# Seven products instead of eight for the last eight blocks of the down-projection

## The chip, the cores and the metric

The kernel runs on one core of a Trainium2 chip. The metric is the device time of one launch in microseconds (us); the cost of an edit is read from one profiled execution. The engines are TensorE (PE in the profile, PEld for its weight loads), VectorE (DVE), ScalarE (ACT), GpSimd (POOL) and SyncE (SP). SP computes nothing: it issues nearly all transfers of the stretch discussed here, in order, and waits in front of each until what it needs is done.

## The reference

A one-layer decoder trunk on 1024 tokens of width 1024. The change lies in the last matrix product, its operand preparation and the final norm.

```python
def conv_ffn(xn, w_up, conv_w, conv_b, w_down):
    u = xn @ w_up                                  # (1024, 5632)
    ...                                            # causal depthwise conv, width 3
    gate, val = jnp.split(c, 2, axis=-1)
    return (jax.nn.silu(gate) * val) @ w_down      # (1024, 2816) @ (2816, 1024)
...
x = x + conv_ffn(rmsnorm(x, norm_ffn_w), ...)
return rmsnorm(x, norm_final_w)
```

## The kernel before

Activations lie transposed: 128 channels on the partitions, tokens along the free axis, in two halves of 512 tokens (`hf`). The hidden layer has NF = 22 blocks of 128 channels; the down-projection sums over these 22 blocks into eight output tiles of 128 channels (`m`), kept in SBUF as `x3` with the residual already in it.

Every fp32 product is made of three matmuls in the fp32r format: an operand is split into a high part (a cast on ScalarE, line L799 for activations, L145 or L122 for weights) and a low part (a subtraction on VectorE, L800, L147, L123), and high x high, high x low and low x high are added in PSUM. So each operand costs one ScalarE and one VectorE instruction, and each block product of 512 tokens three matmuls.

Where eight blocks can be paired into 2 x 2 quarters (output tiles m and m+4, token halves 0 and 1), the kernel replaces eight quarter products by seven, with sums of operands (`product`, L873 to L888). The weight sums S1 to S4 are made by GpSimd from two loaded tiles (`sum_pair`, L98 to L104), the differences T1 to T4 of the activations by VectorE (`sums_h`, L1016 to L1022).

`down` has three stretches, in program order:

1. Blocks 0 to 5 directly (matmuls of L1118).
2. Blocks 6 to 13 in seven products. A first pass over m = 0 to 3 makes A11 B11 into a PSUM tile `y` and A12 B21 (lines L880, L882, L886 to L888, called in L1144 and L1145). A second pass over the same m makes S1 T1, S2 T2, S4 B22, A22 T4 and S3 T3, twelve matmuls each; S2 T2 and S3 T3 are added on top of `y`, and between those two VectorE must read `y` (L1158), because its two partial sums go to different places.
3. Blocks 14 to 21 directly (`mms`, L1091): all eight m for half 0, then for half 1; the last two m of half 1 in quarters of 256 tokens. After each product `evac` adds it to `x3` (L1178), squares it (L1181), sums the squares (L1183) and multiplies by the norm's weight (L1184); `last_norm` makes the final norm.

The order of work is the program's, engine by engine: each engine runs its instructions strictly in the order in which they stand. A tile pool with n buffers makes a load wait until the tile n places before it has been read. Important pools: `hr` (raw activations, 9 buffers), `h` (split activations, 28), `raw` (raw weights, 3), `wh`, `wl`, `sh`, `sl` (split weights, 2 each) and the PSUM tiles `d` and `y` (4 each). Split activations of the last eight blocks are made during the second pass, four for each m (`load_h`), and weights are loaded two items ahead of their use (`next_w`).

Of the kernel before, what the change touches and what calls it, by code (L numbers as in the profile page):

```python
# [17 lines left out]
P = 128  # L18
# [12 lines left out]
N1 = 6  # L31
LPAD, RPAD = 288, 480
# [11 lines left out]
class Trunk:  # L44
# [24 lines left out]
    def ahead(self, n):  # L69
        while len(self.wq) < n and self.wsrc and (self.wsrc[0][1] != "pair" or self.uw):  # L70
# [4 lines left out]
            elif nk == "rest":  # L75
                self.sums["A22"] = self.load_w(src[1][:, 4:8], 4)
                self.wq.append(self.sums)
            elif nk == "pair":
# [28 lines left out]
    def split_pair(self, g, v, sa, sb, skip=0, end=4):  # L107
# [22 lines left out]
        self.pin, self.after = False, None  # L130
        return ops
# [74 lines left out]
    def run(self):  # L206
        nc, tc = self.nc, self.tc
        with ExitStack() as ctx:
# [21 lines left out]
            self.hd = self.dp.tile([NF, P, T], F32, name="hd")  # L230
            self.yd = self.dp.tile([8, P, T], F32, name="yd")
# [15 lines left out]
    def plan(self):  # L247
# [21 lines left out]
        n, n2 = N1 // 2, NF - N1 - 8  # L269
# [6 lines left out]
        src += [(self.w_dn[m, :, N1 + 8:, :], n2) for _ in range(2) for m in range(KC)]  # L276
# [595 lines left out]
    def product(self, ps, a, b, ks=range(4), first=True, last=True, skip=False, low_last=False):  # L872
# [4 lines left out]
        if low_last:  # L877
            for n, k in enumerate(ks):
                for i, x in enumerate(self.B[b, k]):
                    nc.tensor.matmul(ps, ah[:, k, :], x, start=first and n == i == 0, stop=False, skip_group_check=skip)  # L880
            for n, k in enumerate(ks):
                i = nc.tensor.matmul(ps, al[:, k, :], self.B[b, k][0], start=False, stop=last and n == len(ks) - 1, skip_group_check=skip)  # L882
            return i
        for n, k in enumerate(ks):
            bh, bl = self.B[b, k]
# [184 lines left out]
    def down(self):  # L1070

        nc, tc = self.nc, self.tc
        with ExitStack() as ctx:
# [64 lines left out]
            assert not preps  # L1138
            ys = []
# [10 lines left out]
            late = [(hf, j) for hf in range(2) for j in range(N1 + 8, NF)]  # L1150
            for m, y in enumerate(ys):
# [16 lines left out]
                for _ in range(4):  # L1168
                    hf, j = late.pop(0)
                    self.load_h(j, hf)  # L1170
            acc = self.tl(self.uw, [P, 2, H2], "sh")
            js = range(N1 + 8, NF)
            q = H2 // 2

            def evac(ps, m, hf, a=0, b=H2):

                x = x3[:, m, hf * H2 + a:hf * H2 + b]
                tt(x, x, ps, ALU.add)  # L1178
                sum_ = acc[:, hf, a:b]
                sq = sum_ if m == 0 else self.tl(self.uw, [P, b - a], "sl")  # L1180
                nc.scalar.activation(sq, x, AF.Square)  # L1181
                if m and (m < KC - 1 or not hf):
                    tt(sum_, sum_, sq, ALU.add)  # L1183
                nc.scalar.mul(x, x, self.vecs[:, C_NO + m:C_NO + m + 1])  # L1184
                return sq

            tail = []
            for hf in range(2):
                for m in range(KC if hf == 0 else KC - 2):
# [116 lines left out]
```

## Time and profile before

| | |
|---|---|
| median of 3 runs (lowest to highest) | 1350.27 us (1348.31 to 1350.51) |
| profiled execution, its own time | 1349.12 us |
| its span | 1347.3 us |
| PE busy | 1328.9 us, 99% of the span |
| VectorE, ScalarE, GpSimd busy | 77%, 46%, 35% |
| first pass, blocks 6 to 13 | 1170.78 to 1192.37 us |
| second pass | 1192.37 to 1246.94 us |
| last eight blocks, first matmul | 1246.94 us |

The span is the time between the first and last instruction; 1.8 us lie around it. The granted TensorE clock is full. A busy PE in these pages means that matmuls follow each other without a gap; the time of a stretch is then the number of its matmuls times their spacing, and only a change in that number, or a wait that opens a gap, moves the end.

### The profile page before, as it was taken

How to read it: one execution, taken by the hardware profiler on the slowest of the kernel's cores; microseconds unless marked ns; L12 is line 12 of the kernel's file. 1: busy time of each engine (PE TensorE's matmuls, PEld its weight loads, DVE VectorE, ACT ScalarE, POOL GpSimd, SP SyncE). 2: the span in 40 equal slices, each digit the busy share in tenths (PEclk: the TensorE clock that was granted, in tenths of full speed). 3: DMA queues.
4: the chain of work that ended last, by engine and by line, in shares of the span. 5: the costliest groups of instructions: out<-in, count | busy, mean ns of one | idle time of the engine just before them, and what ended most of it. 6: DMA issues, size and time to landing. Idle time of an engine off the chain costs nothing.

```text
span 1347.3 us, 17300 instructions
## 1 busy us (share of the span) xinstructions
PE 1328.9 (99%) x6304; PEld 1104.6 (82%) x6304; DVE 1036.0 (77%) x1557; ACT 616.1 (46%) x1003; POOL 470.6 (35%) x349
## 2 busy tenths in 40 slices
PE   7999999999999999999999999999999999999997
PEld 6888888888888777878888888888888888888887
DVE  7847775289899875465678999999999987986454
ACT  8432232276667665333454444444444434433343
POOL 0336552000102124641455555565555511231011
PEclk9999999999999999999999999999999999999998
DMA  6423443866553235334433222222222238552342
GB/s 257 146 105 150 148 156 141 251 175 188 141 149 130 87 114 207 129 110 155 141 107 96 79 79 94 78 94 74 83 94 74 86 136 315 197 180 67 94 138 81
DMA packets 62468, 179.48 MB, mean 133 GB/s; under 512 B 6832, under 2 KB 15152, under 8 KB 62384
## 3 DMA queue, kind: packets, MB, share of 16 engines
q1 hardware_dynamic: 50928, 160.98, 36.9%
q10 hardware_dynamic: 11456, 17.41, 3.5%
q8 instruction: 49, 0.80, 0.2%
q14 instruction: 35, 0.29, 0.1%
HBM read 129.61 MB, written 48.76 MB: 132 GB/s over the span
## 4 chain that ended last, share of the span: by engine, by line
PE 88%; POOL 4%; DVE 3%; DMA 3%; ACT 1%; issue 1%; POOLq 0%; SPq 0%; ACTq 0%; DVEq 0%
PE t L886 13%; PE t L887 13%; PE t L888 13%; PE y L1091 3%; PE d L1091 3%; PE t L880 3%; PE g L180 3%; PE sc L602 3%; PE g L181 3%; PE g L182 3%; PE y L1118 2%; PE d L1118 2%; DMA gr<-gd 2%; PE sc L182 2%; PE sc L181 2%; PE sc L180 2%
## 5 line engine op out<-in xcount | busy, mean ns | idle before, releaser
L1049 ACT ACTIVATE c<-us,vecs 128x512 f32<-128x512 f32 x80 | 61.3, 780 | 132.5 <-POOL us L1043 128.5
L1051 DVE SCALAR_TENSOR_TENSOR c<-us,vecs,c 128x512 f32<-128x512 f32 x160 | 110.4, 748 | 8.6 <-ACT c L1049 8.6
L145 ACT CAST wh<-raw 128x1024 fp32r<-128x1024 f32 (+2 forms) x60 | 60.8, 1013 | 107.6 <-PE sc L181 30.5
L1043 POOL TENSOR_TENSOR us<-us,rstd 128x1024 f32<-128x1024 f32 x38 | 99.6, 2641 | 4.5 <-DVE us L435 2.4
L147 DVE TENSOR_TENSOR wl<-raw,wh 128x1024 fp32r<-128x1024 f32 (+2 forms) x60 | 75.0, 1250 | 33.3 <-ACT wh L145 21.8
L123 DVE TENSOR_TENSOR sl<-sf,sh 128x1024 fp32r<-128x1024 f32 x62 | 87.5, 1413 | 11.5 <-ACT sh L122 11.5
L122 ACT CAST sh<-sf 128x1024 fp32r<-128x1024 f32 x62 | 63.4, 1048 | 60.4 <-PE t L887 44.2
L123 DVE TENSOR_TENSOR wl<-raw,wh 128x1024 fp32r<-128x1024 f32 (+1 forms) x35 | 74.2, 2120 | 3.7 <-ACT wh L122 3.6
L98 POOL TENSOR_TENSOR sf<-rv 128x512 f32<-128x512 f32 x30 | 41.2, 1375 | 100.6 <-DVE sl L123 57.9
L180 PE MATMUL g<-xh,wh 128*128 128x512 f32 x176 | 70.6, 401 | 0.1
L182 PE MATMUL g<-xh,wl 128*128 128x512 f32 x176 | 70.3, 400 | 0.0
L181 PE MATMUL g<-xl,wh 128*128 128x512 f32 x176 | 70.3, 399 | 0.0
L197 POOL TENSOR_TENSOR rs<-ms,mhalf 128x8 f32<-128x8 f32 (+2 forms) x9 | 14.5, 1607 | 157.7 <-DVE ms L195 147.1
L103 POOL TENSOR_TENSOR sf<-raw,rv 128x512 f32<-128x512 f32 x30 | 40.7, 1356 | 65.4 <-DVE sl L123 65.4
L606 DVE CUSTOM_DVE_ANT_0 L<-sc,bias 128x128 f32<-128x128 f32 (+7 forms) x64 | 47.7, 751 | 17.0 <-PE sc L602 13.9
L585 POOL MEMSET aT<- 128x128 f32 x32 | 6.1, 204 | 151.6 <-PE t L631 101.3
L607 ACT ACTIVATE L<-L,sm 128x128 f32<-128x128 f32 (+7 forms) x64 | 49.6, 778 | 20.0 <-DVE sm L606 17.3
L760 POOL TENSOR_TENSOR gr<-gr,rstd 128x1024 f32<-128x1024 f32 x16 | 41.2, 2583 | 41.7 <-DMA gr<-gd 41.5
L123 DVE TENSOR_TENSOR wl<-rv,wh 128x512 fp32r<-128x512 f32 x30 | 49.3, 1642 | 3.5 <-ACT wh L122 3.5
L1053 ACT ACTIVATE c<-c 128x512 f32<-128x512 f32 x40 | 24.0, 600 | 60.8 <-DVE c L1051 60.8
L602 PE MATMUL sc<-u,u 128*128 128x512 f32 (+2 forms) x192 | 49.6, 358 | 0.0
L182 PE MATMUL sc<-mh,wl 128*128 128x512 f32 x126 | 49.1, 390 | 0.3 <-DVE wl L147 0.3
(515 smaller groups left out, 4334.7 us busy)
## 6 DMA issues: line engine op xcount, KB each, us to landing
u<-qd SPq DMA_DIRECT2D x72, 256.0 KB, 6.5
raw<-in_w_down SPq DMA_DIRECT2D x27, 512.0 KB, 3.6
raw<-in_w_in SPq DMA_DIRECT2D x25, 512.0 KB, 4.2
hr<-hd SPq DMA_DIRECT2D x50, 256.0 KB, 5.4
raw<-in_w_up SPq DMA_DIRECT2D x23, 512.0 KB, 3.5
hd<-c SPq DMA_DIRECT2D x22, 512.0 KB, 2.6
rv<-in_w_up SPq DMA_DIRECT2D x21, 512.0 KB, 3.5
gr<-gd SPq DMA_DIRECT2D x16, 512.0 KB, 3.6
```

The costliest lines, as they stand in the source:

```text
L123: j = nc.vector.tensor_tensor(lo, src, hi.bitcast(F32), ALU.subtract)
L147: self.lo = (eng or nc.vector).tensor_tensor(wl, raw, wh.bitcast(F32), ALU.subtract)
L180: nc.tensor.matmul(ps, wh[:, kc + o, :], ah, start=first and n == 0, stop=False)
L181: nc.tensor.matmul(ps, wh[:, kc + o, :], al, start=False, stop=False)
L182: nc.tensor.matmul(ps, wl[:, kc + o, :], ah, start=False, stop=last and n == len(kcs) - 1)
L602: nc.tensor.matmul(sc[:, lo + n0:lo + n1], qs, k[c][part][:, n0:n1], start=part == 0, stop=part == 1)
L886: nc.tensor.matmul(ps, ah[:, k, :], bh, start=first and n == 0, stop=False, skip_group_check=skip)
L887: nc.tensor.matmul(ps, ah[:, k, :], bl, start=False, stop=False, skip_group_check=skip)
L888: i = nc.tensor.matmul(ps, al[:, k, :], bh, start=False, stop=last and n == len(ks) - 1, skip_group_check=skip)
L1043: (nc.vector if j == 0 else nc.gpsimd).tensor_tensor(u[:, 2:], u[:, 2:], self.rstd, ALU.mult)
L1051: nc.vector.scalar_tensor_tensor(c, u[:, o + k:o + k + H2], col(m, k), c, ALU.mult, ALU.add)
L1091: nc.tensor.matmul(ps, v[:, n, :], x, start=n == i == 0, stop=n == len(js) - 1 and i == 2)
```

## The change

Blocks 14 to 21 are now also made by seven products, as pairs of neighbouring blocks (2k and 2k+1 of the eight). It does so in three passes over m = 0 to 3, and not in two:

- pass one: A11 B11 into `y` and A12 B21 (24 matmuls for each m), which complete half 0 of output tiles 0 to 3;
- pass two: S2 T2, A22 T4, S3 T3 (36 for each m), which complete half 0 of tiles 4 to 7;
- pass three: S1 T1 and S4 B22 (24 for each m, called `fifth` and `third`), which complete half 1. For m = 2 and 3 it runs in quarters of 256 tokens. `third` adds into the PSUM tile that `fifth` left and `evac` has read.

The T1 to T4 of these blocks are made by GpSimd during the group before (`diffs`): four loads, four subtractions, four stores to a scratch tensor `td` in DRAM for each of four k. They come back as ordinary loads (`ready`). The weight sums of pass two are made by GpSimd (`second_pair`) while pass one and two run; S1 and S4 go to a scratch tensor `sd` and come back for pass three. The sums of squares use two activation slots (`slot`) instead of weight tiles.

```diff
+            def diffs(k):
+                b11, b12, b21, b22 = (self.raw_h(N2 + 2 * k + o, hf) for o in range(2) for hf in range(2))
+                for to, x, y, n in ((b11, b12, b11, "T1"), (b12, b22, b12, "T3"), (b22, b22, b11, "T2"), (b21, b22, b21, "T4")):
+                    nc.gpsimd.tensor_tensor(to, x, y, ALU.subtract)
+                    nc.sync.dma_start(self.td[k, TS.index(n)], to)
...
                 if sums:
                     sums.pop(0)()
+                if m > 1:
+                    diffs(m - 2)
-            late = [(hf, j) for hf in range(2) for j in range(N1 + 8, NF)]
+            more = [lambda k=k, n=n, o=o: block(n, k, o, 0) for n, o in (("B11", 0), ("B21", 1)) for k in range(4)]
+            more += [lambda: box.append(slot()) for _ in range(2)]
+            more += [lambda k=k, n=n: ready(n, k) for n in ("T2", "T4", "T3", "T1") for k in range(4)]
+            more += [lambda k=k: block("B22", k, 1, 1) for k in range(4)]
...
-                for _ in range(4):
-                    hf, j = late.pop(0)
-                    self.load_h(j, hf)
+                if m < 2:
+                    diffs(m + 2)
+                prepare(4)
...
+            for m in range(4):
+                w = [x.rearrange("p (k a) c -> p a k c", a=2) for x in self.next_w()]
+                y, ps = bank(1), bank(0)
+                ys.append(y)
+                self.product(y, [x[:, 0] for x in w], "2B11", skip=True, low_last=True)
+                self.product(ps, [x[:, 1] for x in w], "2B21")
+                tt(col(m, 0), col(m, 0), y, ALU.add)
+                evac(ps, m, 0)
+                prepare(3)
+            for m, y in enumerate(ys):
+                w = self.next_w()
+                self.product(y, w["S2"], "2T2", first=False, skip=True)
+                tt(col(m, 1), col(m, 1), y, ALU.add)
+                ps = bank(0)
+                self.product(ps, w["A22"], "2T4")
+                tt(col(m + 4, 0), col(m + 4, 0), ps, ALU.subtract)
+                self.product(y, w["S3"], "2T3", first=False, skip=True)
+                evac(y, m + 4, 0)
+                tt(col(m + 4, 1), col(m + 4, 1), y, ALU.add)
+                prepare(4)
...
+            def fifth(m, w, a=0, b=H2):
+                ps = bank(0)[:, :b - a]
+                self.product(ps, [x[:, 0:4] for x in w], "2T1", skip=True, cols=slice(a, b))
+                evac(ps, m + 4, 1, a, b)
+                return ps
+            def third(m, w, ps, a=0, b=H2, last=False):
+                self.product(ps, [x[:, 4:8] for x in w], "2B22", first=False, skip=True, cols=slice(a, b))
+                return evac(ps, m, 1, a, b, last)
+    def second_pair(self, src, m):
...
+        tt(sa[:, 0], v[:, 0], v[:, 1], ALU.add)
+        tt(sb[:, 0], sa[:, 0], g[:, 0], ALU.subtract)
+        tt(sb[:, 1], g[:, 0], v[:, 0], ALU.subtract)
+        tt(sa[:, 1], g[:, 1], sb[:, 0], ALU.subtract)
+        nc.sync.dma_start(self.sd[m], sa.rearrange("p a k c -> p (a k) c"))
```

In the rows below, numbers behind names tell buffers apart, and line numbers of the changed kernel lie higher.

**SP, where the weights of the second pass for m = 1 are loaded.** Before, `raw_10494` and `raw_10496` are the two tiles from which GpSimd sums S1 to S4 for m = 1; the `hr` loads ahead of them are raw activations of the last eight blocks.

```order
L135 DMA raw_10461<-in_w_down 128x512
L1000 DMA hr_10703<-hd 128x512
L1000 DMA hr_10708<-hd 128x512
L1000 DMA hr_10713<-hd 128x512
L1000 DMA hr_10812<-hd 128x512
L93 DMA raw_10494<-in_w_down 128x1024
L95 DMA raw_10496<-in_w_down 128x1024
```

Now the two tiles are `raw_10528` and `raw_10530`, and the stores of GpSimd's differences (L1179) stand around them.

```order
L1179 DMA td<-hr_10512 128x512
L99 DMA raw_10528<-in_w_down 128x1024
L1179 DMA td<-hr_10514 128x512
L1179 DMA td<-hr_10518 128x512
L1179 DMA td<-hr_10516 128x512
L101 DMA raw_10530<-in_w_down 128x1024
```

A little further on SP, `hr_10646` and `hr_10651` are raw activations of block pair B11 of the last eight blocks, and `raw_10656` and `raw_10658` the weights for m = 2.

```order
L1179 DMA td<-hr_10620 128x512
L1179 DMA td<-hr_10622 128x512
L1179 DMA td<-hr_10626 128x512
L1179 DMA td<-hr_10624 128x512
L1035 DMA hr_10646<-hd 128x512
L1035 DMA hr_10651<-hd 128x512
L99 DMA raw_10656<-in_w_down 128x1024
L101 DMA raw_10658<-in_w_down 128x1024
```

The first weight tile of m = 1 now stands behind one store of k = 1, the second behind all four, and the four stores for k = 2 stand between it and the next activations.

**VectorE, in the second pass at m = 0.** `y` read by L1158 (now L1225) is what S3 T3 waits for. Before:

```order
L123 TENSOR_TENSOR wl_10513<-raw_10496,wh_10512 128x512
L800 TENSOR_TENSOR h_10700<-hr_10698,h_10700 128x512
L800 TENSOR_TENSOR h_10705<-hr_10703,h_10705 128x512
L1156 TENSOR_TENSOR x_9783<-x_9783,d_10516 128x512 x2
L800 TENSOR_TENSOR h_10710<-hr_10708,h_10710 128x512
L800 TENSOR_TENSOR h_10715<-hr_10713,h_10715 128x512
L1158 TENSOR_TENSOR x_9783<-x_9783,y_10298 128x512
L123 TENSOR_TENSOR sl_10505<-c_10498,sh_10504 128x1024
```

Now:

```order
L129 TENSOR_TENSOR wl_10547<-raw_10530,wh_10546 128x512
L1223 TENSOR_TENSOR x_9785<-x_9785,d_10550 128x512 x2
L835 TENSOR_TENSOR h_10648<-hr_10646,h_10648 128x512
L835 TENSOR_TENSOR h_10653<-hr_10651,h_10653 128x512
L1225 TENSOR_TENSOR x_9785<-x_9785,y_10300 128x512
L129 TENSOR_TENSOR sl_10539<-c_10532,sh_10538 128x1024
```

The order of kinds is nearly the same; what is new is which loads the two splits ahead of L1225 read: `hr_10646` and `hr_10651`, which SP issues behind the stores of k = 2.

**VectorE, in pass two of the last eight blocks.** There was no such pass before. L1268 is the read of `y` between S2 T2 and S3 T3; `sl_11216` and `wl_11220` are weights of the next m, `sl_11289` those after it.

```order
L159 TENSOR_TENSOR sl_11216<-c_11209,sh_11215 128x1024
L1250 TENSOR_TENSOR h_10878<-h_10878,h_10879 128x512
L159 TENSOR_TENSOR wl_11220<-raw_11206,wh_11219 128x512
L1268 TENSOR_TENSOR x_9785<-x_9785,y_10992 128x512
```

The same order stands at each m: the split of the next m's weight sums is ahead of the read of this m's `y`.

107 lines of the change are left out of this document (78 added, 29 removed).

## The prediction

> **What bounds the kernel now.** The page first: does any engine but TensorE matter?
>
> ```profile
> span 1347.3 us, 17300 instructions
> PE 1328.9 (99%) x6304; PEld 1104.6 (82%) x6304; DVE 1036.0 (77%) x1557; ACT 616.1 (46%) x1003; POOL 470.6 (35%) x349
> ```
>
> TensorE is busy for 99% of the span. Whether that holds where the change lies, the chain that ended last tells, from 1160 us on (start, length, engine, tile, line, number):
>
> ```profile
> 1170.78 1.81 PE y L880 x8
> ...
> 1246.94 5.44 PE d L1091 x24
> 1252.38 5.44 PE y L1091 x24
> ...
> 1319.53 5.44 PE y L1091 x24
> 1324.97 2.87 PE d L1091 x24
> ...
> 1336.00 1.81 PE y L1091 x15
> 1337.83 0.43 DVE x L1178
> ```
>
> From 1170.78 to 1337.8 us the chain is matmuls without a gap: 24 in 5.44 us, so 0.2267 us for one of 512 columns, and 24 of 256 columns in 2.87. Behind the last one lie 9.5 us of norm and store, whose instructions the change leaves as they are. The waits of TensorE, longest first, agree:
>
> ```profile
> PE t L306 <- ACT wh L145: 7.0, 1, 7.0
> PE g L180 <- DVE gr L779: 1.5, 2, 0.9
> ```
>
> Beyond the start, no line of matmuls waits for more than 1.5 us in all. So fewer matmuls shorten the run by their full time, as long as operands come in time. Each wait that opens a gap is paid in full.
>
> **What it removes.** Blocks 14 to 21 took 8 tiles x 2 halves x 8 blocks x 3 = 384 matmuls of 512 columns (or their equal in quarters). Seven products take 4 x 7 x 4 x 3 = 336. The 48 fewer, at 0.2267 us, are **-10.9 us**. The quarters of the last two m keep their number (96 of 256 columns).
>
> **What it adds beside TensorE.** Three windows before, beside the first pass, the second pass and the last blocks (busy us and count of PE, PEld, DVE, ACT, POOL; clock; DMA share):
>
> ```profile
> 1170.00:1180.00 10.00, 10.00 (x46) 8.29 (x45) 10.00 (x17) 5.32 (x9) 0.00 (x0) 1.00 0.72 228
> 1190.00:1200.00 10.00, 10.00 (x46) 8.28 (x45) 10.00 (x11) 5.02 (x9) 5.92 (x4) 1.00 0.40 133
> 1250.00:1260.00 10.00, 10.00 (x46) 8.29 (x45) 3.89 (x5) 4.62 (x6) 0.00 (x0) 1.00 0.19 53
> ```
>
> VectorE gets 12 more splits, 16 more reads of PSUM and less weight splitting, some 16 us more, in stretches where it was 39% busy after 1250. As load this is hidden. What is not hidden is order: GpSimd gets 32 new subtractions and additions, and SP 20 stores and 20 loads of their results, in queues where others wait behind them. The prices of the steps, from the timeline (GpSimd, VectorE, SP) and from the groups after 1160 us (two ScalarE casts, one VectorE split):
>
> ```profile
> 1190.84 1.75 POOL L103 TENSOR_TENSOR c<-raw,raw 128x512 f32<-128x512 f32 x1
> 1203.21 1.30 POOL L98 TENSOR_TENSOR c<-raw 128x512 f32<-128x512 f32 x1 [7.22 <-DVE sl L123]
> 1191.95 4.59 DVE L800 TENSOR_TENSOR h<-hr,h 128x512 fp32r<-128x512 f32 x3
> 1197.67 1.28 DVE L800 TENSOR_TENSOR h<-hr,h 128x512 fp32r<-128x512 f32 x2
> 1171.26 3.33 SPq L1000 DMA_DIRECT2D hr<-hd  x4
> 1170.55 0.68 DVE L1019 TENSOR_TENSOR hr<-hr,hr 128x512 f32<-128x512 f32 x1
> 1172.35 2.49 DVE L800 TENSOR_TENSOR h<-hr,h 128x512 fp32r<-128x512 f32 x4
> 1203.25 0.39 PE L886 MATMUL y<-h,sh 128*128 128x512 f32 x1
> L799 ACT CAST h<-hr 128x512 fp32r<-128x512 f32 x23 | 13.4, 620 | 11.2 <-DVE hr L1019 7.7 <-PE y L882 1.6 <-PE y L888 1.4
> L122 ACT CAST sh<-c 128x1024 fp32r<-128x1024 f32 x8 | 8.4, 1054 | 23.1 <-PE y L887 18.6 <-POOL c L102 3.8 <-POOL c L104 0.6
> L123 DVE TENSOR_TENSOR sl<-c,sh 128x1024 fp32r<-128x1024 f32 x8 | 10.2, 1275 | 1.0 <-ACT sh L122 1.0
> ```
>
> So a GpSimd step takes 1.30 us alone and up to 1.75 beside VectorE; a VectorE split 0.64 alone and 1.53 beside GpSimd. Transfers, from issue to landing: `hr` loads of 256 KB between 1160 and 1200 us, over the whole run, and weights of 512 KB after 1160:
>
> ```profile
> DMA to landing us min/median/max: 2.7/3.9/7.5
> hr<-hd SPq DMA_DIRECT2D x50, 256.0 KB, 5.4
> raw<-in_w_down SPq DMA_DIRECT2D x24, 512.0 KB, 3.6
> ```
>
> A store is not in these rows alone; I take it as hidden, since each is read long after.
>
> **First wait: S3 T3 of m = 0 in the second pass.** Before, it starts at 1203.25. It needs VectorE's read of `y` (now L1225), which stands behind the splits of `hr_10646` and `hr_10651`; SP issues these two behind the stores of the differences for k = 2. Followed from the front:
>
> - k = 0: its second operand takes the buffer freed at L1019 and goes out at 1171.3 (the SP row), the fourth after two splits of the row at 1172.35, about 1173.6. With 3.9 us they land at 1175.2 and 1177.5. Four GpSimd steps (1.6 us each, as VectorE is full there): 1182.4.
> - k = 1: three of its loads stand behind those stores. The one needed first goes out at 1183.3 and lands at 1187.2; four steps beside a half-free VectorE, 1.5 each: 1193.3.
> - `raw_10530` stands behind the four stores: out at 1193.8, landed at 1197.4.
> - Then GpSimd has eight steps, four weight sums for m = 1 and four differences for k = 2. VectorE is by then short of work, so 1.45 each: 1209.0.
> - Last store, `hr_10646`, `hr_10651` (0.45 us each to issue): 1210.0, landed 1213.9. Cast 0.62, split 0.64, read of `y` 0.6: **1215.8**.
>
> TensorE stands from 1203.25 to 1215.8: **+12.5 us**. Queued with it on VectorE and ScalarE is the split of S1 and S2 for m = 1 (1.05 and 1.28 us behind), but S3 T3 (2.72 us) covers that. With 2.7 us for each landing and 1.30 for each step the read ends at 1208.8 (+5.5); with 5.4 and 1.75 at 1224.5 (+21).
>
> **Second wait: S4 B22 of m = 1**, 8.16 us of matmuls after that. Its weights `sh_10542` stand on ScalarE behind the cast of `hr_10769`, which SP issues behind the store of the first difference for k = 3. GpSimd does that difference behind two weight sums for m = 2, whose buffer comes free at the split of S1 and S2. Counted from the end of the read above: 1.2 (split), three steps 4.2, two issues 0.9, landing 3.9, cast 0.62, cast of S3 and S4 1.05, its low part with two reads ahead of it 2.0: 13.9, less 0.5 as the low part is needed at the third matmul: 13.4. Against 8.16: **+5.2** (3.0 with fast rows, 8.6 with slow ones). After this the orders line up again: the sums for m = 2 and 3 come some 3 to 8 us early by the same count.
>
> **Third: pass two of the last eight.** At each m the read of `y` stands behind the split of the next m's sums. Those take two loads behind the former store (0.8 and 3.9 us) and four GpSimd steps (5.2 to 7.0): a period of 10 to 11.6 us, against 36 matmuls, 8.16 us. The first of these starts when pass one's m = 0 has freed a weight tile. Counted from the start of the last eight: 5.4 for that, casts and splits to 7.7, load to 11.8, four steps to 17.5, second load to 22.4, three steps to 26.5, split 2.4, two VectorE instructions and the read 2.0: 31, where S3 T3 wants to start at 27.2 (120 matmuls). The next two add the difference of the periods where it is not yet waited out. **+6 us** over three m (+1 to +10).
>
> **Pass three** has its weights early (S1 and S4 are back by the end of pass two), and each `third` waits for the read of a `fifth` that ended a product earlier: 1.44 us in the quarters against a read of 0.42. I take 0, with 1.5 us as the upper end.
>
> **Sum**: -10.9 + 12.5 + 5.2 + 6 = **+12.8 us**. Against the profiled execution's 1349.12 us this is 1361.9; the median of the runs shown is 1.15 us higher, so 1363.
>
> **A rule that would add to it.** The start of the run shows what TensorE does after a long rest:
>
> ```profile
> 8.85 0.63 PE L306 MATMUL t<-xh,wh 128*128 128x512 f32 x1
> 9.27 0.63 PE L307 MATMUL t<-xl,wh 128*128 128x512 f32 x1
> 9.70 0.63 PE L308 MATMUL t<-xh,wl 128*128 128x512 f32 x1
> ...
> 13.07 0.39 PE L306 MATMUL t<-xh,wh 128*128 128x512 f32 x1
> 13.30 0.39 PE L307 MATMUL t<-xl,wh 128*128 128x512 f32 x1
> ```
>
> After 7.0 us of waiting, matmuls came 0.42 us apart, and only past 12 us 0.23 apart: over five us, some 2.4 us lost. The same after the first wait would be swallowed by the second, which ends when its own chain ends. After the second and third it would be paid: up to +4.8. The Trainium skill, "TensorE: Matmul & The Clock Gate" (section on the HAM clock gate), states just this: half rate after an idle window of about 3.4 us, until about 3.4 us of work have passed. By that figure I would estimate 1.7 us a wait, and the sum would be 3.4 us more; the trace has one such rest only.
>
> **The rivals.**
>
> 1. *The forecast*, waits by queue order: 1363 us. 70%.
> 2. *Waits that also cool TensorE*, or splits that GpSimd slows where I counted them alone (1.53 against 0.64 us): +3 to +9 more, 1366 to 1372. For it: both rows above. Against: a wait swallows what comes before it. 17%.
> 3. *The gain stands* (faster, 1339 to 1347). If loads land in 2.7 us and GpSimd runs alone at 1.30, the waits shrink to 5.5 + 3.0 + 1, and the net is -1.4: 1349. To be faster by over 0.2% the waits must stay under 8.2 us in all, for instance if SP's loads go out ahead of the stores, or if the split ahead of the read isn't late; with no wait at all it is 1339.4. For it: VectorE, GpSimd and the DMA engines are half idle after 1200 us, so no engine's load forbids it. Against: sixteen GpSimd steps and three landings follow one another before L1225, and at the lowest prices they still end at 1208.8, past 1203.25. It decides there. 6%.
> 4. *Fast rows, partly* (within 0.2%): 1348 to 1353. 7%.
>
> Within 0.2%, 2.7 us, is about what a measurement of this kernel cannot tell from no change. The range leaves out the fast end and the far slow end: 1355 to 1372. Faster 0.06, same 0.07, slower 0.87.
>
> **What would show it.** In the profile after: the two longest waits of TensorE on `y` behind VectorE's read (the line of L1225) and on `sh` behind ScalarE, in the second pass; SP waiting for GpSimd in front of the stores; no wait in the last quarters; the last eight blocks' matmuls counting 336. Were TensorE still 99% busy in the second pass, step one would be wrong and the time near 1340.

## The result, and the profile after

The changed kernel takes 1372.01 us (median of 4 runs, 1370.15 to 1373.67) against 1349.29 us for the kernel before on the same chip (1347.69 to 1350.51). The ratio is 1.0169, with a 95% interval of 1.0147 to 1.0190: slower, as forecast, but by 22.7 us where the sum of the prediction gave 12.8, and past the range by a hundredth of a microsecond. The profiled execution took 1370.15 us, the fastest of the four; its span is 21.0 us longer than before.

The page after, span and TensorE's row:

```profile
span 1368.3 us, 17402 instructions
PE 1326.7 (97%) x6256; PEld 1099.2 (80%) x6256; DVE 1059.8 (77%) x1589; ACT 621.9 (45%) x1019; POOL 516.4 (38%) x381
```

There are 48 matmuls fewer, yet TensorE's busy time fell by 2.2 us only, where 48 at 0.2267 us are 10.9: some matmuls became slower. The waits of TensorE after 1160 us (total, times, longest):

```profile
PE y L921 <- DVE x L1225: 10.6, 2, 10.3
PE y L921 <- DVE x L1268: 7.8, 2, 5.9
PE d L923 <- DVE sl L129: 1.5, 1, 1.5
PE d L219 <- DVE h L1250: 1.1, 1, 1.1
PE y L915 <- ACT wh L176: 1.1, 1, 1.1
PE y L917 <- DVE wl L178: 1.1, 2, 0.8
```

The first three are the three places of the prediction. The others were not in it: L219 sums squares in the final norm, and the last two lie in the first pass, where steps of VectorE became longer beside GpSimd's first differences (1.77 us here, 0.68 for the same step before):

```profile
1177.33 5.31 POOL L1178 TENSOR_TENSOR hr<-hr,hr 128x512 f32<-128x512 f32 x3 [0.92 <-DMA hr<-hd]
1178.01 1.77 DVE L1054 TENSOR_TENSOR hr<-hr,hr 128x512 f32<-128x512 f32 x1
```

What the read and the products behind the longest wait did, from the timeline:

```profile
1216.03 0.68 DVE L1225 TENSOR_TENSOR x<-x,y 128x512 f32<-128x512 f32 x1
1216.76 0.79 PE L921 MATMUL y<-h,sh 128*128 128x512 f32 x1 [10.35 <-DVE x L1225]
1217.35 0.63 PE L922 MATMUL y<-h,sh 128*128 128x512 f32 x1
```

The second product starts 0.59 us behind the first, the rest 0.43 us apart instead of 0.23, 12 in all. The windows by stage say the same with the granted clock (the column behind POOL's counts), first around this wait, then over these 12 products, then around the wait in pass two:

```profile
1204.00:1218.00 14.00, 3.65 (x14) 2.73 (x13) 7.78 (x10) 2.18 (x3) 5.62 (x4) 0.67 0.62 206
1216.80:1222.00 5.20, 5.20 (x12) 4.08 (x13) 3.45 (x4) 0.62 (x1) 3.44 (x3) 0.50 0.78 284
1290.00:1304.00 14.00, 8.06 (x26) 6.14 (x25) 7.26 (x10) 3.44 (x5) 8.68 (x7) 0.76 0.37 131
```

Slow products are products at half the clock. Before, TensorE was busy in every microsecond of the first and the last of these windows, at a clock of 1.00. Where the time went, counted from the starts of matmuls in the timelines of both (the 1170.78 and 1246.94 us given for the kernel before are times of its chain; the matmuls there start at 1170.61 and 1246.77):

| stretch | before, us | after, us | difference |
|---|---|---|---|
| up to the first pass | 1170.61 | 1170.48 | -0.1 |
| first group (first and second pass of blocks 6 to 13) | 76.16 | 95.19 | +19.0 |
| last eight blocks, to the start of the last matmul | 90.74 | 92.29 | +1.5 |
| behind it | 9.81 | 10.37 | +0.6 |

The +1.5 of the last eight blocks is -10.9 for the matmuls and +12.4 for what pass two lost.

The chain that ended last shows the path through both places. In the first group, from the differences for k = 1 to those for k = 2 (start, length, who):

```profile
1188.97 1.92 POOL hr L1178
1190.97 1.30 POOL hr L1178
1192.34 1.63 POOL hr L1178
1193.99 0.32 SPq L1179
...
1194.40 3.87 DMA raw<-in_w_down
...
1198.34 1.29 POOL c L104
...
1205.03 1.73 POOL hr L1178
...
1208.52 1.27 POOL hr L1178
1209.81 0.32 SPq L1179
```

GpSimd's difference (L1178), SP's store (L1179), the load behind the store, GpSimd's weight sum (L104) on what was loaded, the next difference. No row of the chain between 1152.2 and 1235.6 us is of TensorE. In pass two, from one pair's sums to the next:

```profile
1284.90 5.33 DMA raw<-in_w_down
...
1296.44 4.29 DMA raw<-in_w_down
1300.89 1.28 POOL c L149
1302.17 1.69 POOL c L151
1303.86 1.25 POOL c L150
1305.18 1.31 POOL c L152
1306.51 0.33 SPq L153
1306.93 4.83 DMA raw<-in_w_down
...
1316.20 1.05 ACT sh L158
1317.24 0.54 ACT h L1248
1317.81 0.73 ACT x L1252
1318.54 0.68 DVE h L1250
1319.22 0.61 DVE x L1268
```

Load, four sums, store, load: 10.5 us a pair, from 1296.44 to 1306.93. The last five rows were not in the prediction: the read of `y` (L1268) was released through ScalarE, whose cast of the next pair's sums (L158) stands ahead of the squares (L1248) on which VectorE's add (L1250) waits, and the read stands behind this add.

### The profile page after: what moved, and what is told of

It reads as the page before. It is cut to its first block, busy times and chain, and to the rows that moved or that the text cites. A ratio compares the mean times of both kernels' runs of the same rounds, so it can differ in the third digit from the quotient of the medians.

```text
span 1368.3 us, 17402 instructions
## 1 busy us (share of the span) xinstructions
PE 1326.7 (97%) x6256; PEld 1099.2 (80%) x6256; DVE 1059.8 (77%) x1589; ACT 621.9 (45%) x1019; POOL 516.4 (38%) x381
## 4 chain that ended last, share of the span: by engine, by line
PE 77%; POOL 7%; DMA 6%; DVE 5%; issue 2%; ACT 1%; SPq 0%; POOLq 0%; ACTq 0%; DVEq 0%
PE t L922 12%; PE t L923 12%; PE t L921 12%; PE t L915 3%; PE sc L637 3%; PE g L211 3%; PE g L212 3%; PE g L213 3%; DMA gr<-gd 2%; PE sc L213 2%; DMA raw<-in_w_down 2%; PE sc L212 2%; PE sc L211 2%; PE d L1153 2%; POOL gr L795 2%
## 5 line engine op out<-in xcount | busy, mean ns | idle before, releaser
L178 DVE TENSOR_TENSOR wl<-raw,wh 128x1024 fp32r<-128x1024 f32 (+2 forms) x50 | 63.0, 1262 | 30.6 <-ACT wh L176 19.1
L176 ACT CAST wh<-raw 128x1024 fp32r<-128x1024 f32 (+2 forms) x50 | 50.1, 1004 | 73.1 <-PE sc L212 30.5
L104 POOL TENSOR_TENSOR sf<-rv 128x512 f32<-128x512 f32 x30 | 41.3, 1376 | 101.3 <-DVE sl L129 57.8
L835 DVE TENSOR_TENSOR h<-hr,h 128x512 fp32r<-128x512 f32 x62 | 49.3, 825 | 27.8 <-ACT h L834 27.6
L834 ACT CAST h<-hr 128x512 fp32r<-128x512 f32 x62 | 36.8, 619 | 63.8 <-DMA hr<-hd 44.5
```

## Experiments

**The theories.** *A*: queue order. GpSimd comes late to its steps, SP's stores wait for it, and loads, splits and reads stand behind these. *B*: TensorE cooled by the waits is a part of the loss of its own. *C*: GpSimd slows VectorE where both work in SBUF. *D*: seven products don't pay by themselves.

The table gives all runs: time, ratio to the kernel before on the same chip with its interval, and two stretches of the profiled execution (the first group, and the last eight blocks to the start of the last matmul; 76.16 and 90.74 before, 95.19 and 92.29 after). Stretches are compared, since the first pass starts up to 3.3 us earlier or later from one execution to the next, ahead of all that the runs change (e5 and e7 change what stands ahead of it, so their stretches leave a part out). A stretch is read from one execution, a time is a median. e1, e6 and e10 leave work out.

| run | us | ratio | first group | last eight |
|---|---|---|---|---|
| e1, no differences | 1349.53 | 1.0014 (1.0005 to 1.0024) | 76.2 | 91.8 |
| e2, stores on GpSimd | 1368.41 | 1.0159 (1.0144 to 1.0174) | 95.1 | 91.9 |
| e3, read before split | 1366.32 | 1.0142 (1.0127 to 1.0157) | 95.8 | 89.5 |
| e4, filled waits | 1374.77 | 1.0215 (1.0193 to 1.0237) | 101.6 | 90.4 |
| e5, early, own buffers | 1386.12 | 1.0287 (1.0268 to 1.0307) | 87.5 | 89.2 |
| e6, seven products bare | 1336.67 | 0.9920 (0.9905 to 0.9935) | 76.8 | 79.9 |
| e7, early, shared buffers | 1373.73 | 1.0199 (1.0180 to 1.0217) | 90.2 | 92.6 |
| e8, pass two prefetched | 1363.20 | 1.0119 (1.0104 to 1.0134) | 96.3 | 86.1 |
| e9, VectorE's differences | 1355.66 | 1.0064 (1.0045 to 1.0082) | 81.8 | 90.5 |
| e10, stores alone | 1354.27 | 1.0044 (1.0030 to 1.0059) | 79.5 | 91.9 |
| e11, pass two, GpSimd stores | 1366.03 | 1.0135 (1.0120 to 1.0150) | 95.8 | 89.9 |
| e12, e9 and e11 | 1353.13 | 1.0043 (1.0030 to 1.0056) | 81.3 | 89.0 |
| e13, pass two filled | 1366.97 | 1.0135 (1.0120 to 1.0150) | 95.9 | 90.3 |
| e14, ScalarE's order | 1351.15 | 1.0025 (1.0013 to 1.0037) | 80.6 | 87.9 |
| e15, spread differences | 1353.37 | 1.0034 (1.0023 to 1.0045) | 82.2 | 87.7 |
| e16, sums stored by GpSimd | 1348.50 | 1.0010 (1.0001 to 1.0019) | 78.6 | 87.7 |
| e17, adds behind reads | 1345.58 | 0.9986 (0.9977 to 0.9996) | 80.7 | 81.2 |

### What the parts are worth

**e1**: the calls of `diffs` go, and `ready` loads a block:

```diff
-                r = self.tl(self.hrp, [P, H2], "hr")
-                nc.sync.dma_start(r, self.td[k, TS.index(n)])
-                self.B["2" + n, k] = self.parts_h(r)
+                self.B["2" + n, k] = self.parts_h(self.raw_h(N2 + 2 * k, 0))
```

> The changed kernel without GpSimd's sixteen differences and their sixteen stores in the first group; each of the sixteen operands T1 to T4 of the last eight blocks is a half block loaded from the hidden rows instead, so loads and splits stay as many. The sums of the weights in pass two stay. Theory (in-order queues): the waits of 10.35 and 1.45 us, the 2.5 us of slow products behind the first and the 3.3 us of the slower first pass all go, and the 12 us of pass two stay: 1370 to 1372 less 17 to 19, so 1352 to 1355 us. Rival (the splits themselves are too much for VectorE and ScalarE in the first group, whoever makes the sums): a wait of over 4 us stays at the first S3T3 and the time is 1358 or more. Rival (seven products are slower by themselves): the first group is back at its old 80 us but the time stays over 1358.

**e6**: as e1, and in `second_pair` the four sums and the store go:

```diff
+        sb = g
-        tt(sa[:, 0], v[:, 0], v[:, 1], ALU.add)
...
-        nc.sync.dma_start(self.sd[m], sa.rearrange("p a k c -> p (a k) c"))
```

> The changed kernel without either chain on GpSimd: the sixteen differences are left out as before (a half block of the hidden rows is loaded in place of each), and in pass two the weight sums are left out too: S2 and S3 are split from the loaded weights, the store of the other two sums goes, and pass three loads weights of the input in their place. All products, splits, reads and loads of the new scheme stay. Theory (the scheme's 48 fewer products are worth 10.9 us, and all the loss is in the two chains): 1347 to 1349 less 10.9 plus 0.75 at the end: 1337 to 1340 us. Rival (reads and splits of the new order bound it as well): waits stay in pass two or three, 1342 to 1348.

Without the differences the first group is back at 76.16 us, to the hundredth as before, and the time is 2.5 us below what was expected; without the sums as well the kernel is 11.0 us faster than before (1347.64 to 1336.67), and the last eight blocks take 10.9 us less, the 48 matmuls. e6's longest wait of a product after 1160 us:

```profile
PE y L911 <- DVE wl L172: 0.4, 1, 0.4
```

So D falls: the scheme is worth what was counted, and everything lost is lost to the two chains of GpSimd.

### The first group: who holds whom

**e2**: `nc.sync.dma_start(self.td...)` becomes `nc.gpsimd.dma_start(...)`.

> The changed kernel with the sixteen stores of the differences issued by GpSimd behind each difference instead of by SyncE; nothing else is moved and nothing left out. Theory (SyncE's queue): the loads behind the stores start as soon as a buffer is free, VectorE reads y about 10 us earlier, the wait of 10.35 us falls to under 2 us and its 2.5 us of slow products go; the 3.3 us of the first pass and pass two stay: 1357 to 1361 us. Rival (GpSimd's pace or the nine load buffers hold the loads, not the queue): the wait stays over 5 us and the time over 1364. Rival (issuing takes GpSimd's own time): the differences come later and waits move to the last operands of the first group or of pass one; 1362 to 1368.

The theory in that form was wrong and both rivals were seen: the first group lost the same 19 us, in other places (a 5.4 us wait in the first pass, 6.0 at S3 T3). GpSimd's timeline shows a step of 1.3 us turn into one of 2.2 with its own issue behind it:

```profile
1179.15 1.30 POOL L1178 TENSOR_TENSOR hr<-hr,hr 128x512 f32<-128x512 f32 x1
1180.75 0.56 POOL L1179 DMA_DIRECT2D td<-hr  x1 [0.30 <-POOL hr L1178]
```

SP, now without stores, waits for the nine load buffers instead, six loads in 7.34 us:

```profile
1178.84 7.34 SPq L1035 DMA_DIRECT2D hr<-hd  x6
```

**e5 and e7** move the differences to the first six blocks, where GpSimd is idle. In e5 GpSimd loads and stores them itself, with four buffers of its own (HR becomes 5); in e7 only their place changes:

```diff
-                if m > 1:
-                    diffs(m - 2)
...
+                if i in (3, 5, 7, 11):
+                    diffs((3, 5, 7, 11).index(i))
```

> The changed kernel with GpSimd's differences moved ahead, to the stretch of the first six blocks (after the third, fifth, seventh and last piece), where GpSimd is idle for some 50 us; their loads and stores are issued by GpSimd, and they have four buffers of their own, taken from the nine of the loads. Nothing is left out. Theory (GpSimd's differences stand ahead of its weight sums and hold the load buffers in which SyncE's queue is stuck): first pass and second pass of the first group come back to about 80 us, 19 us less; pass two keeps its 12: 1352 to 1355 us. Rival (five buffers are too few for the loads of the splits): new waits of 3 to 12 us in the first six blocks or in the first group, 1356 to 1366. Rival (splits on VectorE and ScalarE are the bound there): the wait at the first S3T3 stays, 1368 or more.

> The changed kernel with the place of the differences alone moved: after the fourth, sixth, eighth and last of the pieces of the first six blocks; loads and stores stay on SyncE's queue and in the nine shared buffers. Nothing is left out. Theory (place on GpSimd's queue decides, since GpSimd is idle there): the first group comes back to about 80 us and what SyncE's queue loses falls where splits are ahead of need: 1352 to 1358 us. Rival (the queue and the nine buffers decide wherever the differences stand): waits of 5 to 15 us move to the first six blocks, 1360 to 1370.

Neither theory held: the waits moved ahead, as the rivals had said, and cost more than the 1366 and 1370 us that these allowed (e5's other rival, splits as the bound, fits the time, but the wait at the first S3 T3 fell to 3.9 us). In e5 GpSimd's last but one step for hidden rows (L1095) stood behind differences that waited for their loads and started at 1144.59 instead of 1124.74, the last at 1165.38 instead of 1143.37, and the first pass began at 1197.68 instead of 1170.48. e5 changed place, queue and buffers at once, so what each of them cost is not shown. In e7 the waits moved into the first six blocks (9.1 us for one cast of weights) and the first pass (4.8). A quiet engine is not a free place: what runs there holds the same queues and buffers.

**e9 and e10** leave everything in its place. e9 lets VectorE subtract (`nc.gpsimd.tensor_tensor` to `nc.vector.tensor_tensor` in `diffs`), e10 drops the subtraction and keeps all 48 transfers.

> The changed kernel with VectorE in place of GpSimd for the sixteen differences, in the same places; stores, loads and buffers stay. Nothing is left out. Theory (what holds the shared load buffers and SyncE's stores is how late GpSimd comes to a difference, behind its weight sums and at 1.3 us each): VectorE needs 0.68 us each, 11 us in all in a stretch of 80 us in which it has some 20 us to spare; most of the 19 us goes, a few us of waits stay: 1354 to 1360 us. Rival (stores in SyncE's queue and the nine buffers cost the same whoever subtracts): 1366 to 1372. Rival (VectorE becomes the bound): waits on VectorE's splits spread over first and second pass, 1360 to 1370.

> The changed kernel with the sixteen differences left out and all else of them kept: the four loads of each, the sixteen stores (of the loaded rows as they are) on SyncE's queue, and the sixteen loads back. Theory (GpSimd's lateness is the cause, not the traffic): SyncE's stores wait for loads alone, some 2 to 4 us each time, and the first group loses at most 4 us: 1352 to 1357 us. Rival (the extra 48 transfers in SyncE's queue and through nine buffers are the cause): half or more of the 19 us stays, 1361 or more.

Both theories held, in time too. The transfers alone cost the first group 3.3 us; VectorE's differences 5.7 us in all, GpSimd's 19.0. So 13 us come with GpSimd as the maker: a difference that it reaches late keeps four of nine buffers and the store in front of SP's loads. One takes it 1.45 us in the median against VectorE's 0.68, it reaches them behind its weight sums, and it slowed VectorE in the first pass (3.0 us). How the rest divides between pace and place in its queue is not shown. e9's waits in the first group:

```profile
PE y L921 <- DVE x L1225: 2.0, 1, 2.0
PE d L923 <- DVE sl L129: 1.5, 1, 1.5
```

### Cooling

**e4 and e13** put spare products of operands already there into the waits, e4 in both stages, e13 in pass two alone:

```diff
+                fill(w["A22"], "2T4", (24, 0, 8, 0)[m])
                 self.product(y, w["S3"], "2T3", first=False, skip=True)
```

> The changed kernel with spare products of operands already there, into a bank that nobody reads, put into three waits of TensorE: 42 ahead of S3T3 of m=0 in the first group, 24 and 8 ahead of S3T3 of m=0 and m=2 in pass two. The computation is whole. Theory (cooling): the waits end when they did, but the 12, 12 and 8 products behind them run at 0.227 us instead of 0.427 us, so 6.4 us less with 74 matmuls more: 1364 to 1366 us. Rival (the slow products are slow for another reason, operands that arrive one by one or a busy port): they stay at 0.43 us and the time is 1370 to 1373, or more where the spare products run past the end of a wait.

> The changed kernel with spare products (into a bank that nobody reads) in two waits of pass two alone: 24 ahead of S3T3 of m=0, 8 ahead of S3T3 of m=2. The computation is whole; the first group is untouched. If cooling is paid as time (4.15 us of slow products on the path): 1366 to 1368.5 us. If GpSimd's chain sets the end of each wait whatever TensorE does in between: the products behind the waits run at 0.227 us, but a wait of 1 to 2 us appears at m=1, the one at m=2 grows, and only the 1.6 us behind the last wait are gained: 1369.5 to 1371. If the slow products have another cause: they stay at 0.43 us, 1371 to 1373.5.

In both the products behind a filled wait are 0.34 and then 0.23 us apart, and the granted clock is 1.00 (e13, 1290 to 1304 us, against 0.76 in the changed kernel): a spacing of 0.43 us is a cooled TensorE. What is gained follows the chain. e4 was to gain 6.4 us and came out slower than the changed kernel (1.0215 against 1.0169): the first wait shrank to 0.65 us and the second grew to 8.3 us. A cast of ScalarE had changed its place there too, so its first group says little. In e13 the rest of the order is kept (two sums of GpSimd swap), and three waits stand where two were:

```profile
1298.09 0.50 PE L921 MATMUL y<-h,sh 128*128 128x512 f32 x1 [0.60 <-DVE x L1274]
1307.54 0.50 PE L921 MATMUL y<-h,sh 128*128 128x512 f32 x1 [0.95 <-DVE x L1274]
1318.47 0.50 PE L921 MATMUL y<-h,sh 128*128 128x512 f32 x1 [0.65 <-DVE x L1274]
```

They are 10.2 us a pair apart in the mean, almost as before (10.45). The last eight blocks took 2.0 us less than in the changed kernel, about the 1.6 us of cooled products behind its last wait. The 2.5 us behind its first were hidden in the next. By the ratios the gain is larger, 0.34% or 4.6 us, and the time lies where all cooling would be paid; but the intervals of the two ratios overlap, so between 2 and 4.6 us stays open.

### Pass two: one queue behind the other

**e3** queues the next pair's splits behind VectorE's read of `y`:

```diff
-                w = self.next_w()
+                w = self.next_w(1)
...
-                tt(col(m, 1), col(m, 1), y, ALU.add)
+                i = tt(col(m, 1), col(m, 1), y, ALU.add)
+                with tc.issue_after(i.ins):
+                    self.ahead(1)
```

> The changed kernel with one order changed in pass two: VectorE reads y (the first of its two reads) ahead of the next pair's splits instead of behind them. Nothing is left out. Theory (VectorE's queue): the wait of 5.94 us at S3T3 of m=0 goes; but GpSimd's chain per pair, 10.5 us, is longer than the 8.2 us that TensorE takes for three products, so S2T2 of m=1 waits 2 to 3 us for its split weights in its place: gain 2 to 5 us with the slow products, 1366 to 1369 us. Rival (only the order was at fault): all 12 us of pass two go, 1358 to 1361. Rival (the read is not what S3T3 waits for): no change, 1370 to 1373.

The size was right, the reason not: the wait at S3 T3 of m = 0 stayed (5.5 us), the one of m = 2 fell from 1.9 to 0.5 us.

**e8** loads the second weight of a pair into load buffers during pass one, and makes its sums there. **e11** adds: GpSimd stores its sums, T1 and B22 are split in pass two behind the current read. **e12** is e11 with e9's differences.

> The changed kernel with pass two's chain begun earlier: the second weight of each pair is loaded as two halves into the load buffers that are free by then, so both loads of a pair are issued during pass one; the first pair's sums are made in pass one, and each later pair's splits stand behind the current read of y. Nothing is left out, the first group stays as it is. Theory (GpSimd's chain of load, four steps, store, and VectorE's order set pass two): without the loads in it a pair's chain takes 5.3 us of GpSimd plus 2.3 of split, less than TensorE's 8.2, and the 12.25 us go: 1357 to 1361 us. Rival (splits and reads queue on VectorE all the same): waits of 1 to 3 us per m stay, 1362 to 1367.

> The kernel with the earlier chain of pass two, with three things more: the stores of the weight sums are issued by GpSimd, T1 and B22 of the last eight blocks are loaded and split in pass two (they are wanted in pass three) instead of pass one, and these splits stand behind the current read of y. Nothing is left out; the first group is that of the changed kernel. Theory (the 4.4 us left in pass two were VectorE's read of y behind splits whose loads stood behind SyncE's store of GpSimd's sums): pass two runs without a wait over 0.5 us and without slow products, 5 to 6.5 us less than with the earlier chain alone: 1357 to 1359 us. Rival (another queue takes its place: GpSimd's pace or T1's splits in pass three): 1360 to 1363.

> Both together: pass two without its waits, and VectorE making the sixteen differences in the first group. Nothing is left out. If both theories hold the gains add: 1372 less 12 less 12 to 18, so 1342 to 1348 us, against 1348 of the kernel before. If VectorE's differences leave the waits of the first group, 1354 to 1360. If VectorE becomes the bound there, 1350 to 1358.

e8 halved what pass two lost (last eight blocks 86.1 us, against 92.3 and e6's 79.9) and fell into its rival's range; e11, meant to take the rest, gave part of it back, as the stores on GpSimd's queue delayed its next pair (an idle time of 6.53 us ended by the store at the third pair). What held the read in e11 is ScalarE's row, a cast that waits for GpSimd, with the squares behind it, and VectorE's add behind these:

```profile
1283.29 1.05 ACT L166 CAST sh<-c 128x1024 fp32r<-128x1024 f32 x1 [7.64 <-POOL c L154]
1284.91 0.69 DVE L1257 TENSOR_TENSOR h<-h,h 128x512 f32<-128x512 f32 x1 [6.93 <-ACT h L1255]
```

e12 did not add the gains up either: 1353.13 us, with 81.3 and 89.0 us in its stretches.

**e14** queues these casts behind the squares too (`tc.issue_after(self.scaled.ins)` around the splits) and lets GpSimd write the stored sums into load buffers. **e15** spreads the differences of the first group. **e16** is e14 with GpSimd's own stores and VectorE's differences behind the last read of their step. **e17** is e16 with the adds of the squares behind the next read of `y`, and T1 and B22 in the last three steps of pass two:

```diff
-                    tt(sum_, sum_, sq, ALU.add)
+                    adds.append(lambda: tt(sum_, sum_, sq, ALU.add))
...
+                with tc.issue_after(i.ins):
+                    flush()
```

> The kernel with VectorE's differences and the prefetched pass two, with two things more: ScalarE's casts of a next pair's sums and of T1 and B22 stand behind the squares of the current products instead of ahead of them, and GpSimd writes the two sums that are stored into load buffers, so its next pair does not wait for the store, which SyncE issues again. Nothing is left out. Theory (ScalarE's queue held the squares, these VectorE's adds, these the read of y): pass two runs without waits, some 9 us less than with the two changes before (5.5 of waits, 3.2 of slow products): 1343 to 1346 us, against 1347 to 1349 of the kernel before. Rival (GpSimd's pace of 5.3 us and 2.3 of split behind late loads): waits of 2 to 4 us stay, 1347 to 1351.

> That kernel with VectorE's differences spread out: one set each in the third step of the first pass and in the first three steps of the second pass, instead of two in the first pass and two in the first half of the second. Nothing is left out. Theory (the load buffers held by two sets in a row delay the splits ahead of the first S3T3): the wait there and the slow products behind it, 4.1 us, go: 1339 to 1343 us. Rival (the reloads of T2 come too late behind the last set): a wait of 2 us or more moves to the last step of the second pass or to pass two, 1343 to 1350.

> The kernel with VectorE's differences, the prefetched pass two and ScalarE's order, with two things more: GpSimd issues the stores of its weight sums itself, so that SyncE's loads of T1 do not stand behind them, and VectorE's differences in the second pass stand behind the last read of y of their step instead of ahead of the weight splits. Nothing is left out. Theory (a read of VectorE behind a split whose load stands behind a store that waits for GpSimd): the wait of 5.5 us and the slow products behind it, some 8 us, and the wait of 3.0 us go: 1339 to 1342 us, against 1347 to 1349 of the kernel before. If only one of the two goes: 1343 to 1348. Rival (VectorE and GpSimd are simply too slow for seven products): the waits move and the time is 1349 or more.

> The kernel before this one with VectorE's adds of the squares in pass one and two put behind the next read of y instead of ahead of it, and the loads and splits of T1 and B22 spread over the last three steps of pass two. Nothing is left out. Theory (GpSimd's sums hold up VectorE's operations whose operands are all in SBUF, the add of 4.73 us above all, and the reads of y from PSUM behind them): the wait of 4.9 us and the slow products behind it go, though the held-up add stays long beside them: 7 us less, 1340 to 1343 us, against 1347 to 1349 of the kernel before. Rival (the splits and casts of the next pair are held up in its place): waits of 2 to 4 us elsewhere in pass two, 1344 to 1349. Rival (the long add was a freak of one execution): no change, 1347 to 1350.

e14 freed m = 0 and showed the pattern once more at m = 1: SP's store of the sums waits for GpSimd, loads of T1 stand behind it, their split ahead of the read.

```profile
1275.92 4.25 SPq L158 DMA_DIRECT2D sd<-hr  x2
1286.49 2.68 DVE L844 TENSOR_TENSOR h<-hr,h 128x512 fp32r<-128x512 f32 x2 [5.04 <-ACT h L843]
```

e15 gained nothing. e16 had 78.6 us in the first group (e17, with the same program there, 80.7), but kept a wait of 4.9 us in pass two, of another kind. All three missed the 1339 to 1346 us of their theories, as each wait taken out left another. VectorE's row, and GpSimd's beside it:

```profile
1271.59 4.73 DVE L1260 TENSOR_TENSOR h<-h,h 128x512 f32<-128x512 f32 x1
1271.99 1.29 POOL L154 TENSOR_TENSOR c<-hr,raw 128x512 f32<-128x512 f32 x1
1273.24 1.29 POOL L155 TENSOR_TENSOR c<-raw,hr 128x512 f32<-128x512 f32 x1
1274.49 1.27 POOL L156 TENSOR_TENSOR hr<-raw,c 128x512 f32<-128x512 f32 x1
1276.24 0.68 DVE L1273 TENSOR_TENSOR x<-x,y 128x512 f32<-128x512 f32 x1
```

An add of 0.68 us took 4.73, until the third of these sums had ended. In e17 it again took long (4.14 us), with less behind it:

```profile
1272.18 4.14 DVE L1266 TENSOR_TENSOR h<-h,h 128x512 f32<-128x512 f32 x1
```

Its waits of TensorE after 1160 us:

```profile
PE d L932 <- DVE sl L127: 1.8, 1, 1.8
PE y L930 <- DVE x L1303: 1.0, 1, 1.0
```

The longest waits of products are now 1.8 us (the first group) and 1.0 us; the wait of 4.9 us is gone. That fits the add in front of the read as its cause, though the splits of T1 and B22 moved too; and the long add was no freak of one execution. The time is 1345.58 against 1347.60 us for the kernel before on the same chip: 0.14% less, within the 0.2% that the prediction counted as no change, and not the 1340 to 1343 of the theory. The profiled execution (1342.87) is one of the fastest of twelve that took 1342.29 to 1347.95. Against e1's first group and e6's last eight blocks its stretches are still 4.5 and 1.3 us longer.

## Why the prediction was wrong, step by step

From the predicted 12.8 us to the 21.0 us of the profiled execution, 1.3 are missing in the first group, 6.4 in pass two and 0.6 at the end, and 0.1 comes off ahead of the first pass. The other 1.7 us up to 22.7 lie between this execution and the medians.

- *48 fewer matmuls, -10.9*: right. e6 shows 10.9 in the stretch and 11.0 in the time.
- *First wait, release at 1215.8*: the read ended at 1216.7 by the row at 1216.03 in the timeline (0.68 us). The step was sized right, and by the steps given: difference, store, load, weight sums, difference, store. Its wait was 10.35 us and not 12.5 because TensorE came 3.0 us late itself: GpSimd's first differences slowed VectorE in the first pass, which was in no term (in e9, where VectorE does them, the first pass loses nothing).
- *Second wait, low part ready 13.9 us after that read*: the third matmul, which needs it, went on at 1230.05, 13.3 us after the read, by the queue named. Half of the 5.2 us expected was filled by cooled products, which the prediction had said would be swallowed here; 1.5 us were left as a wait. First group in all: 19.0 us against 17.7, since the 3.0 us lost in the first pass were only in part made up in the two waits.
- *Third, +6 for pass two (+1 to +10)*: the step that failed: the right kind of chain, sized at half, and above its own upper bound. It measured 12.4. S3 T3 of m = 0 was released 33.3 us after the start of the last eight blocks, not 31 (four sums took 6.95 us beside VectorE, the second load 5.3 instead of 3.9): +2.3. The working had a period of 10 to 11.6 us against 8.16, and the trace has two periods of 10.45 up to m = 2, so 4.6 us on top of the first delay, of which the 6 had kept 2.2: +2.4. And some eight products behind the last wait ran at 0.43 us: +1.6. Together 6.3 of the 6.4 us that were missing. The queue was named in part: VectorE's split was ahead of the read, but what ended last was ScalarE's cast and the squares behind it (chain above, e11; in e3, with the read ahead of the split, 5.5 us of the wait stayed).
- *Pass three, 0*: right for its products. The stretch behind the last matmul is 0.6 us longer: an add of squares (L1250) took 1.23 us beside GpSimd, where the last one takes 0.43, and the last two reads and squares stand behind it. That is inside the bound of 1.5.
- *Rival 2, cooling and slowed splits, 1366 to 1372*: the time fell at its upper end. Of its two causes the trace shows both, cooling with 2.0 us in e13's stretch (4.6 by the ratios), slowed VectorE with up to 3.6 (3.0 in the first pass, up to 0.6 at the end). VectorE's busy time rose by 23.8 us where the working had some 16. Cooling behind the last wait should have been a term of the sum, since the rows for it were there.
- *Rival 3, the gain stands if loads go ahead of stores*: even the orders changed in e8 to e17, with VectorE's differences, end 0.14% under the kernel before; in the order as written the read ended 13.5 us after 1203.25, not before. The gain stands when both chains go (e6).

The Trainium skill, "TensorE: Matmul & The Clock Gate" (section on the HAM clock gate), has half rate after an idle window of about 3.4 us until about 3.4 us of work. The trace agrees for the long waits in kind, but the slow stretch is longer here: 12 products at 0.43 us are 5.1 us of work behind 10.35 and behind 5.94 us. Short waits are not so regular, and two of them cooled TensorE too: the 1.86 us at m = 2 were followed by some five products at full rate and then eight at half (clock 0.52 from 1321.5 to 1324.8 us), in e9 2.0 us by some three at full rate and eight at half, and in e14 3.0 us by none.

## What to carry to other kernels

Price a chain that repeats by its period against the engine that it feeds, and add the excess for each repeat up to the last one that is waited for; the first wait is only its start. Follow each read on which TensorE waits back through every in-order queue (VectorE, ScalarE, the DMA queue and the buffers of its loads), because taking out one leaves the next: here stores, buffers, casts, splits and a held-up add, one after the other. And count a slow engine by how long it holds buffers, stores and steps of others, not by its idle share: moving 16 subtractions from an engine busy for 38% to one busy for 77% saved 14 us by the ratios (1.0169 to 1.0064).

## What the runs showed of the hardware

- A VectorE operation with all operands in SBUF can be held up through a whole row of GpSimd operations: the add took 4.73 us in e16 and 4.14 in e17 instead of 0.68, each beside three sums in a row. In the changed kernel a VectorE add that reads PSUM took 0.67 us at 1179.70, in the middle of GpSimd's differences. The Trainium skill, "SBUF — State Buffer" (section "SBUF: two separate sides"), states that the two share a pair of ports by an exclusive lock held for the whole instruction. The trace agrees so far that the add ended only behind the third sum, in both runs; if this lock is the cause, it was not handed over between three GpSimd instructions in succession. No run shows the lock itself.
- Spare products into an unread bank kept TensorE at full rate through waits of 6 and 10 us (clock 1.00 in e13 and e4, products 0.23 us apart behind it, against 0.43), and in e13's stretch they gained about what no later wait swallowed.
- A store issued by GpSimd cost it 0.56 us and 0.3 to 0.4 us of waiting for its own result (e2), against 0.32 us on SP's queue.
